# Attention of a two-layer trunk: a written order for three engines, transposes moved into the projection, work moved to GpSimd

## Chip, cores and metric

The kernel runs on one core of a Trainium2 chip. The metric is device time in microseconds of one execution. PE is TensorE, DVE is VectorE, ACT is ScalarE, POOL is GpSimd and SP the queue that starts the transfers.

## What is computed

One attention layer and one convolution layer, each followed by an MLP, over 1024 latent tokens and 256 context tokens (1280 keys in 10 tiles of 128), width 1024. Only the attention is touched. It has two parts whose outputs are projected together:

```python
def diff_attention(q, k, v, lam, lam_init, subln_g):      # 4 heads, two scores each
    s = jnp.einsum('bqhid,bkhid->bhiqk', q, k) * (HEAD_DIM ** -0.5)
    p = jax.nn.softmax(s.astype(jnp.float32), axis=-1)
    attn = (p[:, :, 0] - lam * p[:, :, 1]).astype(v.dtype)
    o = jnp.einsum('bhqk,bkhe->bqhe', attn, v)
    o = rms_norm(o, subln_g) * (1.0 - lam_init)
...
def gqa_attention(q, k, v):                               # 8 query heads, 2 key heads
    s = jnp.einsum('bqgrd,bkgd->bgrqk', q, k) * (HEAD_DIM ** -0.5)
    p = jax.nn.softmax(s.astype(jnp.float32), axis=-1).astype(v.dtype)
    o = jnp.einsum('bgrqk,bkgd->bqgrd', p, v)
```

## The kernel before

All is float32. Where precision is wanted, an operand is split into a rounded high part and a rest (`split`, `sub` at L78: `lo = a - hi`), and the products are summed in PSUM.

The stages follow each other in time: the projection (`project`, to 268 us of the span), the differential attention (268 to 495, with a tail to 513), the grouped attention (513 to 753), then the output projection and the rest of the trunk to the end.

**Projection.** `swept` and `groups` produce keys, queries and values tile by tile in PSUM; `keys_a`, `queries_a`, `rest_b` and `queries_b` turn each tile by its rotary angles (and norm it, in the grouped heads) on DVE and leave it with the tokens on partitions (`kA`, `qA`, `kB`, `qB`).

**Differential attention.** 32 steps: 4 heads of 8 blocks of 128 queries; two steps are a unit (`UnitA`). Of a head's keys, `kstack` transposes ten tiles twice on PE (L1113), ACT copies the high part (L1115), DVE subtracts for the rest (L78); `qstack` does so for 512 queries (L1128, L1131, L1132). A step computes two rows of scores of 128x1280 in three PSUM banks each (`softmax`: L1142, L1143), takes the maximum on DVE (L1145), the exponentials with their sum on ACT (L1148), combines both on DVE into `e0 + cc * e1` (L1261, 128x1280), transposes ten tiles (`transposed`, L1157, copied by ACT at L1162), and every second step multiplies by the values (L1279). Every fourth step `finish` norms 512 columns of the output: a square, two matmuls (L1290, L1291), and `rsqrt0` with DVE's L468 to L470 and L1296; POOL makes the diagonal operand (L1267).

**Grouped attention.** Eight halves of two heads, called j, each of ten key tiles. Per key tile `exponentials` runs four matmuls (L1388, L1389) and two exponentials (L1390) into `pt`; the sum over tiles is added up by POOL for tiles 1 to 6 and by DVE for 7 to 9 (L1394, 128x1024); `values` runs four matmul records (L1403) two tiles later. `ahead` computes the next j's maxima in eight pieces of three matmuls (L1362) and three reductions (L1364), one piece per tile, and writes each into `w` (L1365), which `shifts` transposes and copies (L1371, L1375, L1377). `divide` sums over partitions on PE (L1418), inverts on ACT (L1421, L1422) and multiplies on DVE (L1423 to L1425).

**Order.** Nothing in these stages is written in engine order: Tile's scheduler places every instruction by the priority in which `build` issues it, moved by `high_priority(offset=...)`. PSUM holds two score tiles of three banks (later five of one bank and the values' own) and two banks named `one` for everything else. Scratch of 128x512 comes from a pool `u` of 23 buffers, exponentials from one of 6.

## Time and profile before

| what | value |
|---|---|
| median of three executions | 2577.77 us (2576.82 to 2579.6) |
| profiled execution | 2576.91 us |
| its span, first to last instruction | 2575.1 us |
| mean granted TensorE clock | 0.974 |
| PE, DVE, ACT, POOL busy, share of the span | 95%, 73%, 48%, 13% |

A row of a list of groups reads: line, engine, operation, output and inputs with their shapes, count, then busy microseconds and mean nanoseconds of one, then idle time of the engine ahead of them and what ended it. A row of a timeline reads: start and duration in microseconds, engine, line, operation, count, and in brackets the idle time before it. Matmuls overlap in the pipeline, so the distance from one start to the next is their cost, and the duration of a group is a little longer than that. PE carries two or four records for a float32 operation of full precision.

### The profile page before, as it was taken

The page shows a single profiled execution, that of the slowest core. Times are in us where ns is not written, and L with a number is a line of the kernel's source. Part 1 is how long each engine was busy: PE and PEld are TensorE (multiplying, and loading weights), DVE is VectorE, ACT ScalarE, POOL GpSimd, SP SyncE. Part 2 cuts the span into 40 slices and gives each one's busy share as a digit, 9 for nine tenths or more (in the row PEclk, how much of TensorE's full clock was granted, in tenths as well). Part 3 has the DMA queues.
Part 4 walks back from the last instruction along what each step waited for, and adds up shares of the span by engine and source line. Part 5 has one row for each costly group of instructions (what it writes and reads, how often), then busy time and mean ns, then how long its engine had stood idle before and what let it go on. Part 6 is the DMA issues. An engine that isn't in the chain of part 4 may idle for free. (4 is left out here: it accounts for less than half of the span.)

```text
span 2575.1 us, 30269 instructions
## 1 busy us (share of the span) xinstructions
PE 2435.0 (95%) x10950; PEld 1895.7 (74%) x10950; DVE 1891.7 (73%) x2925; ACT 1225.9 (48%) x1986; POOL 345.2 (13%) x230
## 2 busy tenths in 40 slices
PE   7999899999999979999899999999999999899997
PEld 5888677744447767787688777788777888688786
DVE  4847888887768787876756689767887565765867
ACT  3113577755542475554344346534258555344343
POOL 0001000044442410000000033001231000000002
PEclk9999899999999989999899999999999999899999
DMA  7811011000011057877542221123213444843231
GB/s 271 288 52 46 21 21 46 15 16 6 1 66 50 21 177 250 258 270 257 197 150 88 94 103 33 58 82 120 102 33 126 141 151 160 308 136 132 88 117 66
DMA packets 118519, 297.15 MB, mean 115 GB/s; under 512 B 13536, under 2 KB 19296, under 8 KB 118368
## 3 DMA queue, kind: packets, MB, share of 16 engines
q1 hardware_dynamic: 118368, 295.20, 34.2%
q8 instruction: 86, 1.41, 0.2%
q14 instruction: 65, 0.53, 0.1%
HBM read 225.29 MB, written 63.96 MB: 112 GB/s over the span
## 5 line engine op out<-in xcount | busy, mean ns | idle before, releaser
L74 PE MATMUL ps<-bl,part 128*128 128x512 f32 x784 | 309.7, 396 | 7.0 <-DVE bl L78 7.0
L73 PE MATMUL ps<-bh,part 128*128 128x512 f32 x784 | 310.4, 397 | 6.2 <-ACT part L916 6.2
L75 PE MATMUL ps<-bh,part 128*128 128x512 f32 x784 | 308.7, 396 | 5.8 <-DVE part L78 5.8
L916 ACT CAST part<-a 128x512 fp32r<-128x512 f32 x196 | 121.7, 623 | 306.5 <-PE ps L74 159.8
L78 DVE TENSOR_TENSOR part<-a,part 128x512 fp32r<-128x512 f32 x196 | 134.7, 690 | 162.1 <-ACT part L916 162.1
L73 PE MATMUL ps<-T,a 128*128 128x512 f32 x608 | 238.6, 392 | 6.4 <-DVE tmp L825 3.6
L74 PE MATMUL ps<-T,a 128*128 128x512 f32 x608 | 237.5, 391 | 2.2 <-DVE T L78 2.2
L75 PE MATMUL ps<-T,a 128*128 128x512 f32 x608 | 237.2, 390 | 0.0
L536 POOL TENSOR_TENSOR acc<-acc,mb 128x512 f32<-128x512 f32 x29 | 48.1, 1688 | 1070.6 <-ACT mb L533 1070.6
L73 PE MATMUL ps<-H,a 128*128 128x512 f32 x456 | 178.5, 392 | 3.7 <-ACT a L540 3.7
L74 PEld LDWEIGHTS ps<-bl,part 128*128 128x128 f32 x784 | 150.2, 192 | 41.1 <-DVE bl L78 9.2
L78 DVE TENSOR_TENSOR a<-raw,a 128x1024 fp32r<-128x1024 f32 (+1 forms) x114 | 119.2, 1047 | 83.3 <-PE ps L74 72.5
L75 PEld LDWEIGHTS ps<-bh,part 128*128 128x128 f32 x784 | 150.3, 192 | 38.7 <-DVE part L78 7.2
L73 PEld LDWEIGHTS ps<-bh,part 128*128 128x128 f32 x784 | 149.8, 191 | 39.3 <-ACT part L916 7.4
L74 PE MATMUL ps<-H,a 128*128 128x512 f32 x456 | 177.9, 390 | 0.0
L75 PE MATMUL ps<-H,a 128*128 128x512 f32 x456 | 177.7, 390 | 0.0
L540 ACT CAST a<-raw 128x1024 fp32r<-128x1024 f32 (+1 forms) x114 | 100.9, 908 | 136.2 <-PE ps L74 94.6
L825 DVE TENSOR_TENSOR tmp<-ps,tmp 128x512 f32<-128x512 f32 x114 | 78.4, 689 | 116.0 <-PE ps L75 80.2
L73 PEld LDWEIGHTS ps<-T,a 128*128 128x128 f32 x608 | 114.4, 188 | 35.3 <-DVE tmp L825 6.2
L74 PEld LDWEIGHTS ps<-T,a 128*128 128x128 f32 x608 | 114.4, 188 | 26.6 <-DVE T L78 3.6
L75 PEld LDWEIGHTS ps<-T,a 128*128 128x128 f32 x608 | 114.6, 188 | 23.9
L1390 ACT ACTIVATE pt<-s 128x512 f32<-128x512 f32 x160 | 92.7, 596 | 81.0 <-PE s L1389 72.1
(414 smaller groups left out, 5907.0 us busy)
## 6 DMA issues: line engine op xcount, KB each, us to landing
gq<-tmp SPq DMA_DIRECT2D x196, 256.0 KB, 3.4
b<-gq SPq DMA_DIRECT2D x98, 512.0 KB, 3.3
raw<-in_w SPq DMA_DIRECT2D x72, 512.0 KB, 4.2
a<-in_w SPq DMA_DIRECT2D x140, 256.0 KB, 5.1
raw<-in_adaT SPq DMA_DIRECT2D x48, 512.0 KB, 5.0
adar<-in_adaT SPq DMA_DIRECT2D x32, 512.0 KB, 5.0
raw<-in_cw_in SPq DMA_DIRECT2D x24, 512.0 KB, 3.6
ada<-in_adaN SPq DMA_DIRECT2D x16, 512.0 KB, 8.4
```

The source lines that it names most:

```text
L73: mm(ps, lhsT=lh, rhs=rh, start=start, stop=False, **kw)
L74: mm(ps, lhsT=lh, rhs=rl, start=False, stop=False, **kw)
L75: mm(ps, lhsT=ll, rhs=rh, start=False, stop=stop, **kw)
L78: return eng.tensor_tensor(out=out, in0=a, in1=hi.bitcast(F32), op=ALU.subtract)
L536: self.eng(NORM[li, h]["sub"][j]).tensor_tensor(out=a, in0=a, in1=mb, op=ALU.subtract)
L540: self.nc.scalar.copy(out=hi, in_=src)
L825: nc.vector.tensor_tensor(out=o, in0=a, in1=b, op=op)
L916: self.tc.keep_in_program_order(nc.scalar.copy(out=hi, in_=src))
L1390: nc.scalar.activation(pt[:, s, :], o, AF.Exp)
```

## The change

1. `keys_a`, `queries_a`, `rest_b` and `queries_b` now transpose their tile at once (`turned`: up to four PE transposes of 128x128 into a bank `one`, and as many ACT copies), 114 transposes in all, into `kT`, `qT`, `kB`, `qB` with the tokens along the row. `kstack` and `qstack`, with 164 transposes, are gone; `keys` and `queries` read SBUF. The rest of a differential key moves from DVE to POOL.
2. From the end of the projection to the end of the attention the order on PE, ACT and DVE is the one in which the code issues (`manual_schedule`).
3. The combination is cut by groups of 512, 512 and 256 columns: DVE does the first, POOL the other two, each as a scaling (TENSOR_SCALAR) and an addition (TENSOR_TENSOR). Steps 30 and 31 stay with DVE.
4. The norms of the differential heads leave that stage. The unscaled output is kept, and each of the eight norms runs during one j of the grouped part, with one float32 matmul instead of two, four small scalings and one addition on POOL for the diagonal, and four DVE instructions.
5. The grouped part goes in rounds of two key tiles; the values of a round stand together in the next one, eight records in a row; one reduction writes all of `w`; the addition of key tile 7 moves from DVE to POOL; the four loads of the first output weights are spread.
6. The buffers: `u` 30 instead of 23, exponentials 7 instead of 6.

The core of the diff:

```diff
+        def turned(src, outs):
+            tr = self.one()
+            for h in range(4):
+                nc.tensor.transpose(tr[:, h * P:(h + 1) * P], src[:, h * P:(h + 1) * P], self.ident)
+            for h in range(4):
+                nc.scalar.copy(out=outs[h], in_=tr[:, h * P:(h + 1) * P])
...
         def queries_a(t, z):
-            rope_to(z, t - NC, 8, [(self.qA[h][:, t - NC, :], h * P, P) for h in range(4)], tmp(), tmp())
+            q = tmp()
+            rope_to(z, t - NC, 8, [(q, 0, 512)], tmp(), tmp())
+            turned(q, [self.qT[h][:, (t - NC) * P:(t - NC + 1) * P] for h in range(4)])
...
+            nc.scalar.copy(out=k1[r, c:c + m * P], in_=a)
+            t.sub(nc.gpsimd, k2[r, c:c + m * P], a, k1[r, c:c + m * P])
...
-        nc.vector.scalar_tensor_tensor(out=e0, in0=e1, scalar=cc, in1=e0, op0=ALU.mult, op1=ALU.add)
+            if g == 0 or n >= 30:
+                nc.vector.scalar_tensor_tensor(out=a, in0=b, scalar=cc, in1=a, op0=ALU.mult, op1=ALU.add)
+            else:
+                nc.gpsimd.tensor_scalar(out=b, in0=b, scalar1=cc, scalar2=1.0, op0=ALU.mult, op1=ALU.mult)
+                nc.gpsimd.tensor_tensor(out=a, in0=a, in1=b, op=ALU.add)
...
+                    for g in (1, 2)[:1 + (k - 3) % 2]:
+                        self.transposes(k - 3, g)
+                        self.copies(k - 3, g)
+                if b:
+                    self.scores(k, 1)
+                if 0 <= k - 1 < n:
+                    self.combine(k - 1)
+                if c:
+                    self.transposes(k - 2, 0)
+                if b:
+                    self.exponentials(k, 0)
+                if c:
+                    self.copies(k - 2, 0)
+                if b:
+                    self.exponentials(k, 1)
+                if k >= 4:
+                    self.values((k - 4) // 2, k % 2)
...
+                for m in range(8):
+                    at(5 * j + m // 2, m % 2, lambda j=j, m=m: self.maximum(j + 1, m // 2, m % 2))
+                later(5 * j + 4, 0, lambda j=j: self.shifts(j + 1), 1)
+            if j < 6:
+                at(5 * j + 2, 2, lambda j=j: self.queries(j + 2))
...
+            later(5 * j + 3, 0, norm, 5, 7, 9)
+            later(5 * j + 6, 2, lambda j=j: self.divide(j), 2, 4)
...
-            eng = nc.gpsimd if kt < 7 else nc.vector
+            eng = self.nc.gpsimd if kt < 8 else self.nc.vector
```

(`at(r, place, f)` puts f behind the first tile, behind the second, or at the end of round r; `later` puts the parts that f returns the given number of places on.)

DVE in the differential attention, a step in mid-stage before. L1145 takes a row's maximum, L1266 and L1258/L1259 make factors of one column, L1261 is the combination, L1132 belongs to `qstack`.

```order
L1132 SCALAR_TENSOR_TENSOR q_3176<-one,q_3176 64x512
L1145 TENSOR_REDUCE mx<-s 128x1 x2
L1266 TENSOR_TENSOR c_3233<-sm 128x1
L1145 TENSOR_REDUCE mx<-s 128x1
L1258 RECIPROCAL cc<-sm 128x1
L1259 SCALAR_TENSOR_TENSOR cc<-cc,sm,nlam 128x1
L1261 SCALAR_TENSOR_TENSOR e<-e,cc 128x1280
```

The same place now (L1158 is the maximum, L1176 the combination, L1144 the queries' rest):

```order
L1176 SCALAR_TENSOR_TENSOR e<-e,cc 128x512
L1144 SCALAR_TENSOR_TENSOR q_4034<-qT_1349,q_4034 64x512
L1144 SCALAR_TENSOR_TENSOR q_4035<-qT_1349,q_4035 64x512
L1158 TENSOR_REDUCE mx<-s 128x1 x2
L1171 RECIPROCAL cc<-sm 128x1
L1172 SCALAR_TENSOR_TENSOR cc<-cc,s_2788,nlam 128x1
```

Both maxima of a step now stand together, the combination has 512 columns instead of 1280, and the queries come from SBUF. POOL there, which had one small L1267 per step before, now (L1178 scales, L1179 adds, L78 is a key's rest):

```order
L78 TENSOR_TENSOR k_2953<-kT,k_2952 64x256
L1178 TENSOR_SCALAR e<-e,cc 128x512
L1178 TENSOR_SCALAR e<-e,cc 128x256
L1179 TENSOR_TENSOR e<-e 128x512
L1179 TENSOR_TENSOR e<-e 128x256
L78 TENSOR_TENSOR k_3016<-kT,k_3015 64x512
```

Two scalings and two additions a step, and in six steps of a head a key's rest, have come to POOL. DVE in the grouped attention, one j, before:

```order
L1423 TENSOR_TENSOR ra<-one,r 128x512
L1365 TENSOR_REDUCE w<-mx_6026 128x1
L1364 TENSOR_REDUCE mx_6049<-s 128x1 x3
L1424 SCALAR_TENSOR_TENSOR r<-ra,r 128x512
L1365 TENSOR_REDUCE w<-mx_6049 128x1
L1425 SCALAR_TENSOR_TENSOR ot<-ot,r 128x512
L1364 TENSOR_REDUCE mx_6087<-s 128x1 x3
L1352 SCALAR_TENSOR_TENSOR q_6062<-one,q_6062 64x512
L1365 TENSOR_REDUCE w<-mx_6087 128x1
L1394 TENSOR_TENSOR e<-e,pt 128x1024 x2
L1377 CAST q_5823<-one 64x512
L1352 SCALAR_TENSOR_TENSOR q_6063<-one,q_6063 64x512
```

And now (L1376 maxima, L1246 to L1249 the norm, L1362 the queries' rest, L1446 to L1448 the division, L1413 the additions):

```order
L1413 TENSOR_TENSOR e<-e,pt 128x1024 x2
L1376 TENSOR_REDUCE mx_5538<-s 128x1 x9
L1246 TENSOR_TENSOR dg<-dg,one 128x512
L1247 TENSOR_SCALAR dg<-dg 128x512
L1248 TENSOR_TENSOR sq<-sq,dg 128x512
L1249 SCALAR_TENSOR_TENSOR ot<-ot,subg,sq 128x512
L1376 TENSOR_REDUCE mx_5538<-s 128x1 x9
L1362 SCALAR_TENSOR_TENSOR q_5672<-qB_2261,q_5672 64x512
L1362 SCALAR_TENSOR_TENSOR q_5673<-qB_2261,q_5673 64x512
L1376 TENSOR_REDUCE mx_5538<-s 128x1 x3
L1446 TENSOR_TENSOR ra<-one,r 128x512
L1447 SCALAR_TENSOR_TENSOR r<-ra,r 128x512
```

The norm stands between the maxima of the third and the fourth piece, in each j; the queries' rest now reads two operands from SBUF. DVE at the end of the attention, before, where `spread` (L202) makes the gate's rows that PE transposes ahead of the output projection:

```order
L1394 TENSOR_TENSOR e<-e,pt 128x1024 x3
L202 COPY spread<-m_63 128x128 x8
L1423 TENSOR_TENSOR ra<-one,r 128x512
L1424 SCALAR_TENSOR_TENSOR r<-ra,r 128x512
L78 TENSOR_TENSOR hl<-ot,hh 128x512
L1425 SCALAR_TENSOR_TENSOR ot<-ot,r 128x512
```

And now:

```order
L1413 TENSOR_TENSOR e<-e,pt 128x1024 x2
L1246 TENSOR_TENSOR dg<-dg,one 128x512
L1247 TENSOR_SCALAR dg<-dg 128x512
L1248 TENSOR_TENSOR sq<-sq,dg 128x512
L1249 SCALAR_TENSOR_TENSOR ot<-ot,subg,sq 128x512
L1446 TENSOR_TENSOR ra<-one,r 128x512
L1447 SCALAR_TENSOR_TENSOR r<-ra,r 128x512
L1448 SCALAR_TENSOR_TENSOR ot<-ot,r 128x512
L202 COPY spread<-m_63 128x128 x8
```

The eight `spread` copies stand behind the last norm and the last division.

## Rows read from the trace of the kernel before

**Rows 1.** Busy time by stage: stretch, length, each engine with its instructions, clock

```profile
268.00:495.00 227.00, 208.89 (x1089) 163.79 (x1088) 197.47 (x273) 171.56 (x306) 16.11 (x36) 0.96 0.11 27
495.00:513.00 18.00, 17.96 (x90) 14.07 (x91) 16.08 (x38) 8.10 (x15) 0.40 (x1) 1.00 0.05 10
513.00:753.00 240.00, 236.59 (x913) 112.80 (x911) 182.59 (x310) 129.57 (x228) 117.44 (x51) 1.00 0.03 10
```

**Rows 2.** Groups by form in the differential attention, 300 to 490 us

```profile
L1145 DVE TENSOR_REDUCE mx<-s 128x1 f32<-128x1280 f32 x54 | 79.9, 1484 | 7.6 <-PE s L1143 7.2
L1148 ACT ACTIVATE e<-s,mx 128x1280 f32<-128x1280 f32 x54 | 71.9, 1332 | 11.9 <-DVE mx L1145 11.1
...
L1261 DVE SCALAR_TENSOR_TENSOR e<-e,cc 128x1280 f32<-128x1280 f32 x27 | 41.9, 1550 | 0.8
```

**Rows 3.** PE's timeline in the differential attention, 380 to 391 us

```profile
381.73 1.02 PE L1291 MATMUL one<-dg,sepsm 128*128 128x512 f32 x2
382.59 1.89 PE L1279 MATMUL one<-pt,vA 128*128 128x256 f32 x8
384.32 0.60 PE L1157 MATMUL one<-ident,e 128*128 128x128 f32 x4
...
388.00 1.06 PE L1157 MATMUL one<-ident,e 128*128 128x128 f32 x8
388.81 0.47 PE L1143 MATMUL s<-k,q 128*128 128x512 f32 x1
...
389.81 0.39 PE L1142 MATMUL s<-k,q 128*128 128x512 f32 x1
...
390.97 0.59 PE L1279 MATMUL one<-pt,vA 128*128 128x256 f32 x2
```

**Rows 4.** Groups by form on POOL, whole span

```profile
L675 POOL TENSOR_TENSOR acc<-acc,y 128x512 f32<-128x512 f32 x11 | 19.0, 1745 | 110.1 <-DVE y L88 110.1
...
L78 POOL TENSOR_TENSOR wlo<-wraw,whi 128x512 fp32r<-128x512 f32 x8 | 10.3, 1300 | 212.7 <-ACT whi L230 212.6
...
L1313 POOL MEMSET w<- 128x512 f32 x2 | 1.0, 526 | 0.0
```

**Rows 5.** PE's timeline at the end of the projection

```profile
246.16 0.64 PE L1113 MATMUL one<-ident,kA 128*64 128x128 f32 x2 [3.99 <-DVE k L78]
```

**Rows 6.** Busy time in the sixth and the eighth j of the grouped attention

```profile
676.00:705.00 29.00, 28.91 (x118) 14.47 (x116) 22.95 (x42) 16.08 (x28) 14.18 (x6) 1.00 0.00 1
...
729.00:753.00 24.00, 24.00 (x96) 9.55 (x94) 11.24 (x14) 12.78 (x24) 14.59 (x6) 1.00 0.07 22
```

**Rows 7.** Groups by form in the grouped attention, 510 to 740 us

```profile
L1394 POOL TENSOR_TENSOR e<-e,pt 128x1024 f32<-128x1024 f32 x37 | 88.6, 2394 | 22.9 <-ACT pt L1390 22.4 <-DVE mx L1364 0.3
...
L1394 DVE TENSOR_TENSOR e<-e,pt 128x1024 f32<-128x1024 f32 x21 | 27.5, 1311 | 1.2 <-ACT pt L1390 0.3
...
L1424 DVE SCALAR_TENSOR_TENSOR r<-ra,r 128x512 f32<-128x512 f32 x6 | 16.3, 2723 | 0.0
```

**Rows 8.** DVE's timeline in the eighth j

```profile
742.15 0.69 DVE L1423 TENSOR_TENSOR ra<-one,r 128x512 f32<-128x512 f32 x1 [12.48 <-ACT r L1422]
742.88 2.79 DVE L1424 SCALAR_TENSOR_TENSOR r<-ra,r 128x512 f32<-128x512 f32 x1
...
752.17 1.17 DVE L202 COPY spread<-m 128x128 f32<-128x128 f32 x8
```

**Rows 9.** POOL's timeline in the eighth j

```profile
742.75 5.16 POOL L1394 TENSOR_TENSOR e<-e,pt 128x1024 f32<-128x1024 f32 x2 [0.18 <-ACT pt L1390]
```

**Rows 10.** PE's timeline in the grouped attention and behind it

```profile
640.46 1.08 PE L1403 MATMUL pv<-pt,vB 128*64 128x512 f32 x4
641.47 0.50 PE L1388 MATMUL s<-q,k 128*128 128x512 f32 x1
...
749.91 2.80 PE L1403 MATMUL pv<-pt,vB 128*64 128x512 f32 x12
...
757.77 2.87 PE L73 MATMUL ps<-hid,wfh 128*128 128x512 f32 x5 [1.71 <-ACT hid L540]
```

More of the change, by code (lines that the diff above doesn't have):

```diff
@@ L450, in project @@
             if t == 3:
-                self.at.units[0].prepare()
+                for s, g in ((0, 0), (0, 1), (0, 2), (1, 0), (1, 1), (1, 2)):
+                    self.at.keys(0, s, g)
+                self.at.queries(0, 0)
         pps.__exit__(None, None, None)
@@ new lines, in transposes, with copies @@
+    def transposes(self, n, g):
+        g0, gn = GROUPS[g]
+        tr = self.tr[n, g] = self.one()
+        for i, m in enumerate((n,) if gn == 4 else (n - 1, n)):
+            for k in range(gn):
+                c = (i * gn + k) * P
+                self.nc.tensor.transpose(tr[:, c:c + P], self.e[m, 0][:, (g0 + k) * P:(g0 + k + 1) * P], self.t.ident)
+    def copies(self, n, g):
+        gn = GROUPS[g][1]
+        pt = self.pt.setdefault(n // 2, [])
+        tr = self.tr.pop((n, g))
+        if gn == 4:
+            if n % 2 == 0:
+                pt.append(self.pl.tile([P, gn, 256], F32, name="pt", tag="pt", bufs=8))
+            self.nc.scalar.copy(out=pt[g][:, :, n % 2 * P:(n % 2 + 1) * P], in_=tr.rearrange("p (k q) -> p k q", q=P))
+        else:
+            pt.append(self.t.ut("pt").rearrange("p (k q) -> p k q", k=gn))
+            self.nc.scalar.copy(out=pt[g].rearrange("p k (i q) -> p k i q", i=2), in_=tr.rearrange("p (i k q) -> p k i q", i=2, k=gn))
@@ new lines, in values @@
+    def values(self, u, half):
+        t, nc = self.t, self.nc
+        h, b = u // 4, u % 4
+        pt = self.pt[u]
+        if half == 0:
+            self.pv = self.one()
+        pv = self.pv
+        for kt in range(half * 5, half * 5 + 5):
+            nc.tensor.matmul(pv[:, 0:256], lhsT=t.vA[kt][:, h * P:(h + 1) * P], rhs=pt[kt // 4][:, kt % 4, :],
+                             start=kt == 0, stop=kt == KT - 1)
+        if half == 1:
+            if b == 0:
+                t.oT.append(t.qo.tile([P, T], F32, name="ot", tag="qo"))
+            nc.scalar.copy(out=t.oT[h][:, b * 256:(b + 1) * 256], in_=pv[:, 0:256])
@@ new lines, in misc @@
+    def misc(self, n):
+        h, i = divmod(n, 8)
+        if i == 0:
+            self.queries(h, 1)
+        if h < 3:
+            for s, g in {1: [(0, 0)], 2: [(0, 1)], 3: [(0, 2)], 4: [(1, 0)], 5: [(1, 1)], 6: [(1, 2)]}.get(i, ()):
+                self.keys(h + 1, s, g)
+            if i == 5:
+                self.queries(h + 1, 0)
+        elif i in (3, 4, 5):
+            if i == 3:
+                self.grouped = Grouped(self)
+            self.grouped.keys(0, i - 3)
+        elif i == 6:
+            self.grouped.queries(0)
+            self.t.w_first = []
+        elif i == 7:
+            self.t.first_weights(0)
@@ L1164, in build @@
     def build(self):
         t = self.t
[L1166 to L1168 removed]
+        self.s0 = self.pl.tile([P, 32], F32, name="s0")
+        self.epsi = self.pl.tile([P, P], F32, name="epsi")
+        self.nc.gpsimd.tensor_scalar(out=self.epsi, in0=t.ident, scalar1=P * EPS, scalar2=1.0, op0=ALU.mult, op1=ALU.mult)
+        n = 32
         psa = t.pool("ps2", space=PSUM)
         self.pp = psa.__enter__()
[L1172 to L1177 removed]
@@ L1201, in build @@
-        for k in range(n + 4):
-            if k == n:
-                psa.__exit__(None, None, None)
-                psb = t.pool("ps3", space=PSUM)
-                self.grouped.pp = psb.__enter__()
-            for f, offset in ((prepare, 200), (weights, 100), (scores, None), (values, 0), (finish, 0)):
-                if offset is None:
-                    f(k)
-                else:
-                    with t.tc.high_priority(offset=offset):
-                        f(k)
-            if k >= n:
-                self.grouped.first(k - n)
@@ new lines, in build @@
+        E = mybir.EngineType
+        with t.tc.manual_schedule(engines={E.PE, E.Activation, E.DVE}):
+            for k in range(n + 4):
+                if k == n:
+                    psa.__exit__(None, None, None)
+                    psb = t.pool("ps3", space=PSUM)
+                    self.grouped.pp = psb.__enter__()
+                a, b, c = 0 <= k - 3 < n, k < n, 0 <= k - 2 < n
+                if b:
+                    self.scores(k, 0)
+                if a:
+                    for g in (1, 2)[:1 + (k - 3) % 2]:
[11 more added lines that the diff above has]
+                    self.copies(k - 2, 0)
+                if b:
+                    self.exponentials(k, 1)
+                if k >= 4:
+                    self.values((k - 4) // 2, k % 2)
+                if b:
+                    self.misc(k)
+                else:
+                    self.grouped.first(k - n)
+            self.grouped.build()
```

430 lines of the change are left out of this document (192 added, 238 removed).

## Prediction

> **What bounds the kernel now.** I read the busy time by stage first. PE is busy for 209 of 227 us in the differential attention, 236.6 of 240 in the grouped one [rows 1]: the second waits for nothing but PE, the first has 18 us of PE idle. Behind the attention the order on PE, POOL and SP stays what it was, so that the time can change only up to some 766 us of the span.
>
> In the groups by form of the differential attention, 54 maxima in 190 us are 27 steps [rows 2], 7.04 us each. Over the stage a step has 6.5 us of PE (208.89 over 32), 6.2 of DVE and 5.4 of ACT [rows 1]. No engine is full: the step is longer than each, since two PSUM buffers of scores go round PE, DVE and ACT, and the maxima idle for PE, the exponentials for the maxima [rows 2].
>
> **The change part by part.** The sum stands against the profiled execution, 2576.9 us; the median of the runs shown is 0.9 higher.
>
> *A, the projection.* 114 transposes of 0.10 us (eight from 388.00 to the next start at 388.81 [rows 3]) are 11.5 us on a PE that is full there. Out go the first head's 28 transposes ahead of its scores, 3, and PE's wait for DVE's rest of a key, 4.0 [rows 5], which now is POOL's. New is that the tiles' transposes wait for DVE's rotation; its price is between 0 (PE works ahead on other tiles) and the 4.0 of the nearest wait [rows 5]. With a little under half of it: +6, between +4 and +9.
>
> *B, the 32 steps.* After the change a step has on PE two times six score matmuls of 1.16 us (389.81 to 390.97), ten transposes of 0.10, and ten value records of 0.216 (eight from 382.59 to 384.32) [rows 3]: 2.32 + 1.0 + 2.2 = 5.5, taken as 5.8 with the switches. On DVE: two maxima of 1.48, 0.62 of the combination (1.55 for 1280 columns, by columns [rows 2]), some 0.6 of small ones and queries: 4.2. ACT stays near 5. On POOL: the addition of 512 columns at 1.30 (two operands, `wlo`) [rows 4], 0.65 for half as many; the scaling is not in the trace, and lies between 0.53, the price of a fill of the same shape, and 1.30 of two operands [rows 4]. I take 0.6, since it reads one operand, and 0.35 for 256. A key's rest is 0.8 per step spread over a head (four of 512 columns and two of 256 in eight steps), and DVE's combination holds POOL up once, 0.6. Together 4.3, between 4.2 and 5.4. PE is then the longest at 5.8. Four filling steps at 5 and 28 at 5.8 are 182 in place of 227: **-45**. The cover is POOL's time below PE's, and that the combination has a step and a half until its transposes.
>
> *C, the stage's end.* DVE works for 16 of the 18 us between the last scores and the grouped part [rows 1], mostly on the first j's maxima. In the written order these stand behind the last two combinations (1.55 each [rows 2]), and `shifts` behind all. +5, between 0 and +8.
>
> *D, the grouped part.* PE first. A j takes 29.0 us, 28.9 of them PE [rows 6]. The values in rows of eight save their switch: four records cost 1.01 alone and 0.86 in a row (a third of 12 records less the overlap) [rows 10], 0.8 in five rounds; the queries' transposes go, 0.4; the norm's mean comes, 0.86 (381.73 to 382.59 [rows 3]). That is 28.6, and 22 in the last j, which takes 24 without maxima [rows 6]. If nothing waits, the part takes 7 x 28.6 + 22 = 222, 18 less.
>
> Then DVE. The eighth j shows a wait that the grouped part will have more of. While POOL adds two tiles, 742.75 to 747.9 [rows 9], DVE's L1424 takes 2.79 for work of 0.69, which is what L1423 took just before [rows 8]. It ends when the first addition of 2.39 has ended: the two take turns, and each DVE instruction waits for a whole one of POOL. L1424 does so in every j: 2.72 in the mean [rows 7], a wait of 2.03. L1423, which reads PSUM and one operand from SBUF, does not wait; those that wait read both from SBUF. Before, five instructions per j are of the kind: the three additions, which come when POOL has finished and take 1.31 [rows 7], and two of the division. Now there are nine: three of the norm, two of the queries' rest (whose first operand was PSUM), two of the division, two additions. POOL has more too: seven additions of 2.39 [rows 7], and the norm's diagonal (four scalings of 128 columns, put at 0.45 each, a third of a two-operand addition of 512, and one addition of 1.30 [rows 4]), 3.1: 19.8 per j in place of 14.2 [rows 6], and its queue is filled from the second round to the last. DVE's own work is 22.95 [rows 6], less one addition of 1.31, less the wait of 2.03, plus four of the norm at 0.69: 22.4, and 22 as `w` takes one reduction for eight. With the share of POOL's work in a j of length j as the chance that an instruction has to wait: j = 22 + 9 x 2.03 x 19.8 / j, so j = 33. Following one j by hand through the written order gives the same: PE waits about 2 us for the fourth piece, whose maxima stand behind the norm, 1 for scores behind the queries, and 3 for `shifts` behind the additions. PE can't go round these waits any more. 7 x 33 + 22 = 253 against 240: **+13**. Bounds are 222 (no wait) and 7 x 40 + 22 = 302 (each of the nine waits).
>
> The Trainium skill ("SBUF — State Buffer", section "Who interferes with whom") says that DVE shares its second pair of SBUF ports with GpSimd, and that whoever issues first gets that pair for the whole instruction while the other fully blocks. Read as arrival at any moment, an instruction would wait half of POOL's, 1.2, and only as often as POOL is busy: 22 + 9 x 0.6 x 1.2 = 28.5, no more than PE's own j. The row of 2.79 shows a whole wait instead, for a POOL with work queued; but it is one place in the j, so this is the first rival.
>
> *E, the end.* The eight `spread` copies (1.17 from 752.17 [rows 8]) ran ahead of the last division and now stand behind it and the last norm; the output projection, which began at 757.77 on ACT's `hid` [rows 10], begins later by these and the transposes behind them. +3, between +1 and +6.
>
> The sum: 6 - 45 + 5 + 13 + 3 = -18, and 2576.9 - 18 = 2559, the forecast.
>
> **The rivals.**
>
> *Waits in the grouped part stay small.* For it: DVE's additions took 1.31 in the mean before [rows 7], so they hardly waited, and DVE has 6 us of slack in a j [rows 6]. Against it: POOL's queue is now full when the queries and the division come. With j = 29.5 (28.6 and a little), D is 7 x 29.5 + 22 - 240 = -11, and the time 2535.
>
> *The turn-taking decides, and the kernel is slower.* The place is DVE's queue between the second and the fourth round, where norm, queries and division come one behind the other while POOL always has an addition waiting: each waits whole. The gain of the other parts, 6 - 45 + 5 + 3 = -31, is used up at 7j + 22 = 271, j = 35.6, so with about 6.7 of the nine waiting. With j = 38 (eight waiting) D is +48, and the time 2594. For it: 742.88 [rows 8]. Against it: turns also slow POOL, so that it empties at the end of a j.
>
> *POOL bounds the differential steps.* L675's additions of 512 columns took 1.75 beside a busy DVE [rows 4]. With this for scalings and additions and half of it for 256 columns, a step has 5.2 + 0.8 + 0.6 = 6.6 on POOL, and 28 steps cost 0.8 more each than forecast: 2559 + 22 = 2581, and 2590 if the keys are as dear.
>
> *The steps don't get shorter.* PE in a written order waits at each place for the latest of POOL's sums, ACT's copies and PSUM's two score tiles. If the 7.04 was the round through the two tiles [rows 2] and not the engines' load, it stays: 28 x 1.24 = 35 more, 2594. Against it: both maxima and exponentials now come without the 1.55 of the combination between them.
>
> **How the numbers follow.** Forecast 0.38, small waits 0.22, turn-taking 0.18, POOL 0.08, no shorter steps 0.14. A difference under 0.2%, 5 us, can hardly be told from none in this kernel. Forecast and small waits together give 0.57 of faster, 0.03 within; of the other 0.40 some 0.06 still end faster, 0.09 within, 0.25 slower. Faster 0.63, same 0.12, slower 0.25. The low end is the forecast with D at no wait (-18 in place of +13) and A and C at their lower bounds: 2576.9 + 4 - 45 + 0 - 18 + 3 = 2521, with a little of B taken as 2518. The high end is that of the two slow rivals, 2596. The forecast's own range is 2545 to 2571.
>
> **What would show it.** Right: a step of 5.8 us between maxima of the same kind, PE over 95% busy there, the first grouped scores near 479 of the span in place of 513; in the grouped part instructions of DVE with 2.0 us over their own time, five or six per j, and PE idle behind the maxima and `shifts`, j of 33. Wrong: a step at 7, with POOL full (rival three) or idle (rival four); a j below 30 with DVE's norm at 0.7 each; a scaling on POOL outside 0.53 to 1.30; an output projection that begins as soon after the last values as before.

## Result and the profile after

The changed kernel takes 2613.85 us in the median of four executions (2607.54 to 2618.66), the kernel before 2577.36 beside it: a ratio of 1.0138, 95% interval 1.0116 to 1.0161. It is slower; the forecast was 2559, its range 2518 to 2596, and the time lies above it. The profiled execution, the fastest of the four, took 2607.54 us with a span of 2605.8, PE busy for 93% of it in place of 95%.

The gain came where it was expected, at half the size, and the loss came in three other places. The bounds are first and last rows: of the maxima of the differential steps, of the grouped scores that feed exponentials (L1405), of the sums over partitions (L1438).

| stretch, us of the profiled span | before | after | difference | forecast |
|---|---|---|---|---|
| A: start to the first maximum | 271.4 | 299.3 | +27.9 | +6 |
| B: first to last maximum | 222.1 | 199.6 | -22.5 | -45 |
| C: to the first grouped scores | 19.1 | 28.2 | +9.1 | +5 |
| D: to the last sum | 240.4 | 258.9 | +18.5 | +13 |
| E: to the end | 1822.1 | 1819.8 | -2.3 | +3 |

The last stretch runs the same instructions in all kernels and came out between 1819.8 and 1830 in the runs below, so that a difference of a few us in it tells nothing, and a time is judged by its ratio.

Busy time by stage, after (columns as in [rows 1], which they answer to):

```profile
100.00:299.00 199.00, 175.37 (x905) 146.72 (x904) 120.59 (x294) 56.55 (x219) 17.57 (x14) 0.96 0.24 74
299.00:499.00 200.00, 179.45 (x969) 152.16 (x968) 151.87 (x183) 149.79 (x265) 135.68 (x149) 0.97 0.11 25
499.00:527.00 28.00, 23.23 (x100) 16.72 (x100) 21.52 (x40) 11.47 (x20) 0.00 (x0) 0.94 0.06 19
527.00:786.00 259.00, 230.17 (x886) 112.80 (x885) 197.27 (x267) 139.84 (x252) 171.59 (x99) 0.95 0.04 11
```

PE, which had next to no idle time in the projection and the grouped part before, now idles for 23.6 us in the first row and 28.8 in the last.

**A.** PE's waits from 100 to 300 us, after (line waited, for what: us in all, times, longest), then the only row for 100 to 272 us before:

```profile
PE one L418 <- DVE tmp L364: 15.1, 8, 5.3
PE one L446 <- DVE tmpk L364: 7.0, 6, 3.0
PE one L418 <- ACT tmp L425: 1.1, 1, 1.1
```

```profile
PE one L1113 <- DVE k L78: 4.0, 1, 4.0
```

These are 15 waits of PE at the new transposes, 23.2 us: 14 for DVE's rotation and one for ACT's copy of a context tile. DVE's timeline of two query tiles before, and then after:

```profile
259.91 0.76 DVE L356 TENSOR_TENSOR tmp<-tmp,rs 128x256 f32<-128x256 f32 x2
260.59 0.68 DVE L383 TENSOR_REDUCE ss<-tmp 128x8 f32<-128x512 f32 x1
261.19 0.68 DVE L358 TENSOR_TENSOR tmp<-tmp,rc 128x512 f32<-128x512 f32 x1
...
264.19 0.76 DVE L356 TENSOR_TENSOR tmp<-tmp,rs 128x256 f32<-128x256 f32 x2
```

```profile
257.68 0.76 DVE L358 TENSOR_TENSOR tmp<-tmp,rs 128x256 f32<-128x256 f32 x2
...
259.20 0.69 DVE L364 TENSOR_TENSOR tmp<-tmp 128x512 f32<-128x512 f32 x1
259.81 0.68 DVE L385 TENSOR_REDUCE ss<-tmp 128x8 f32<-128x512 f32 x1
...
262.18 0.23 DVE L86 SCALAR_TENSOR_TENSOR ssa<-ss,eps,ssa 128x8 f32<-128x8 f32 x1 [1.49 <-ACT ssa L85]
...
263.58 0.76 DVE L358 TENSOR_TENSOR tmp<-tmp,rs 128x256 f32<-128x256 f32 x2
```

Before, the next tile's reduction (L383) stood inside this tile's rotation, and a tile took 4.3 us (264.19 - 259.91). After, it stands behind it, DVE then waits 1.49 for ACT, and a tile takes 5.9. PE, held at the transposes, came late to the first scores (293.01 in place of 268.24):

```profile
285.84 1.09 PE L418 MATMUL one<-ident,tmp 128*128 128x128 f32 x4 [4.51 <-DVE tmp L364]
292.27 1.09 PE L418 MATMUL one<-ident,tmp 128*128 128x128 f32 x4 [5.34 <-DVE tmp L364]
293.01 0.78 PE L1155 MATMUL s<-k,q 128*128 128x512 f32 x1
```

**B.** Eight steps in the middle of the stage, what PE waited for most from 347 to 445 us (16 steps), and POOL's scaling from 300 to 480 us:

```profile
396.10:444.65 48.55, 45.86 (x258) 39.59 (x257) 36.81 (x45) 38.97 (x69) 36.70 (x41) 1.00 0.13 28
```

```profile
PE s L1155 <- ACT e L1164: 4.5, 4, 1.5
```

```profile
L1178 POOL TENSOR_SCALAR e<-e,cc 128x512 f32<-128x512 f32 x28 | 32.7, 1168 | 56.5 <-DVE cc L1172 44.6 <-ACT pt L1198 11.9
...
L1178 POOL TENSOR_SCALAR e<-e,cc 128x256 f32<-128x256 f32 x27 | 13.7, 508 | 0.0
```

A step is 48.55 / 8 = 6.07 us. PE is busy for 5.73 of it (94%) and waits for 0.34, mostly until ACT's exponentials have read a tile of scores. POOL is idle for a quarter of the time. Its scaling of 512 columns took 1.17, but that is not its own time. DVE's combination, which reads two operands from SBUF, starts just ahead of it; a step after the change, and then one of e5 (below) where no combination runs beside the scaling (x2 is the scaling of 512 and of 256 columns):

```profile
399.79 0.75 DVE L1176 SCALAR_TENSOR_TENSOR e<-e,cc 128x512 f32<-128x512 f32 x1
399.86 1.70 POOL L1178 TENSOR_SCALAR e<-e,cc 128x512 f32<-128x512 f32 x2 [0.45 <-DVE cc L1172]
```

```profile
417.21 1.15 POOL L1178 TENSOR_SCALAR e<-e,cc 128x512 f32<-128x512 f32 x2 [0.61 <-DVE cc L1172]
```

The scaling of the 512 columns took 1.25 of the first and 0.69 of the second.

**C.** DVE's maxima of the first j, behind the last two combinations:

```profile
508.72 6.20 DVE L1376 TENSOR_REDUCE mx<-s 128x1 f32<-128x512 f32 x12 [1.88 <-PE s L1374]
...
517.11 6.20 DVE L1376 TENSOR_REDUCE mx<-s 128x1 f32<-128x512 f32 x12 [0.75 <-PE s L1374]
```

**D.** PE's two longest sums of waits in the grouped part, DVE's groups there, and the place where one j hands over to the next on PE:

```profile
PE one L1385 <- DVE w L1379: 13.6, 6, 2.6
PE s L1374 <- DVE mx L1376: 10.2, 8, 1.7
```

```profile
L1248 DVE TENSOR_TENSOR sq<-sq,dg 128x512 f32<-128x512 f32 x7 | 15.4, 2195 | 0.2
L1362 DVE SCALAR_TENSOR_TENSOR q<-qB,q 64x512 fp32r<-64x512 f32 x12 | 13.4, 1113 | 1.5 <-ACT q L1360 1.2
L1448 DVE SCALAR_TENSOR_TENSOR ot<-ot,r 128x512 f32<-128x512 f32 x7 | 12.7, 1811 | 0.2
L1447 DVE SCALAR_TENSOR_TENSOR r<-ra,r 128x512 f32<-128x512 f32 x7 | 10.3, 1472 | 0.2
```

```profile
644.57 1.94 PE L1422 MATMUL pv<-pt,vB 128*64 128x512 f32 x8
...
650.24 0.66 PE L1385 MATMUL one<-ident,w 128*128 128x128 f32 x4 [2.61 <-DVE w L1379]
...
652.28 3.00 PE L1422 MATMUL pv<-pt,vB 128*64 128x512 f32 x8
```

The instructions with two SBUF operands take 0.4 to 1.5 us more than their own 0.69, and the last maxima and `w` stand behind them. L1247, which reads one operand from SBUF, waits too (804 ns, and 427 in e12 below). Behind five of the six waits for `w` PE's clock is lower for a while: here eight value records took 3.00 in place of 1.94.

The values' copies part one j from the next. In the middle of the stage they are 34.2 us apart, the last two 22.7. One j after the change, and then one of e12 (below), where POOL adds no key tiles:

```profile
661.60:695.80 34.20, 29.75 (x115) 14.74 (x116) 27.07 (x37) 17.69 (x33) 21.29 (x13) 0.95 0.00 1
```

```profile
648.90:678.00 29.10, 28.00 (x115) 14.39 (x116) 22.29 (x37) 17.55 (x33) 3.45 (x5) 1.00 0.00 1
```

DVE is busy for 27.1 of the 34.2, 4.8 more than without POOL's additions, and idle for the other 7.1: it is not full.

### The profile page after: what moved, and what is told of

Its sections match the earlier page's. It is cut to its first block, busy times and chain, and to the rows that moved or that the text cites. A ratio compares the mean times of both kernels' runs of the same rounds, so it can differ in the third digit from the quotient of the medians.

```text
span 2605.8 us, 30302 instructions
## 1 busy us (share of the span) xinstructions
PE 2412.5 (93%) x10884; PEld 1892.8 (73%) x10884; DVE 1872.9 (72%) x2761; ACT 1238.0 (48%) x2080; POOL 526.2 (20%) x395
## 5 line engine op out<-in xcount | busy, mean ns | idle before, releaser
L78 DVE TENSOR_TENSOR part<-a,part 128x512 fp32r<-128x512 f32 x196 | 134.8, 690 | 157.5 <-ACT part L921 157.4
L78 DVE TENSOR_TENSOR a<-raw,a 128x1024 fp32r<-128x1024 f32 (+1 forms) x114 | 119.6, 1050 | 82.9 <-PE ps L74 72.6
L73 PEld LDWEIGHTS ps<-T,a 128*128 128x128 f32 x608 | 114.1, 188 | 34.2 <-DVE tmp L830 4.6
L1407 ACT ACTIVATE pt<-s 128x512 f32<-128x512 f32 x160 | 86.8, 595 | 109.7 <-PE s L1406 109.1
L74 PEld LDWEIGHTS ps<-T,a 128*128 128x128 f32 x608 | 114.1, 188 | 27.4 <-DVE T L78 4.3
L74 PE MATMUL ps<-hid,w 128*128 128x512 f32 (+1 forms) x336 | 127.4, 380 | 4.3 <-POOL hid L78 2.4
```

The source lines that it names most:

```text
L73: mm(ps, lhsT=lh, rhs=rh, start=start, stop=False, **kw)
L74: mm(ps, lhsT=lh, rhs=rl, start=False, stop=False, **kw)
L78: return eng.tensor_tensor(out=out, in0=a, in1=hi.bitcast(F32), op=ALU.subtract)
L1407: nc.scalar.activation(pt[:, s, :], o, AF.Exp)
```

## Experiments

**The late tiles' transposes alone** (A). The last four query tiles' transposes move into the second to fifth step.

```diff
-            turned(q, [self.qB[h][:, t * P:(t + 1) * P] for h in range(4)])
+            outs = [self.qB[h][:, t * P:(t + 1) * P] for h in range(4)]
+            if t < 4:
+                turned(q, outs)
+            else:
+                self.at.late.append(lambda: turned(q, outs))
```

> Edit: the transposes of the last four grouped query tiles leave the projection and stand in steps 1 to 4 of the differential attention. Theory one (PE, in order, waits at those transposes for DVE's rotation): the waits of 2.1, 4.5, 5.3 and 2.9 us at L418 go, the first scores start near 282 of the span in place of 293.0, the step and the grouped part stay, and the time falls by 9 to 14, to some 2601. Rival (the chain of the last query tiles through ACT and DVE, 5.9 to 6.4 us a tile, holds the first maxima whatever PE does): the first maximum stays later than 296 of the span, and the gain is under 4.

Ratio 1.013 [1.011, 1.0151]; the first maximum came at 297.0, 2.3 earlier. PE reached its first scores sooner, at 286.59, and waited there 6.30 us in one piece, until just behind DVE's scaling of a query tile (L388, which ended at 294.09; PE went on at 294.19). With these transposes out of the way DVE's chain of query tiles held the start.

**All keys and queries of the grouped part transposed late** (A). They are kept as rows, as before, and transposed in place in the steps.

```diff
-            zn, q = headnorm(z, 8, tmp()), tmp()
-            rope_to(zn, t, 8, [(q, 0, 512)], tmp(), zn)
-            turned(q, [self.qB[h][:, t * P:(t + 1) * P] for h in range(4)])
+            zn = headnorm(z, 8, tmp())
+            rope_to(zn, t, 8, [(self.qB[h][:, t * P:(t + 1) * P], h * P, P) for h in range(4)], tmp(), zn)
...
+        if n >= 4 and n % 8 != 7 and self.late:
+            x, c0, m = self.late.pop(0)
+            tr = self.one()
+            for y in range(m):
+                self.nc.tensor.transpose(tr[:, y * P:(y + 1) * P], x[:, c0 + y * P:c0 + (y + 1) * P], self.t.ident)
+            self.nc.scalar.copy(out=x[:, c0:c0 + m * P], in_=tr[:, 0:m * P])
```

> Edit: grouped queries and keys stay in rows in the projection, as before the change, and are transposed in place in steps 4 to 15 of the differential attention (eleven times up to four transposes and one copy). Theory one (the 42 transposes make PE wait for ACT's and DVE's work on each tile, some 19 us in all, and so delay the next tile's products, which start that work): PE's waits at these lines go, the first maximum comes between 275 and 284 in place of 299, the steps lose 1 to 4, and the time falls by 14 to 22, to about 2596. Rival (DVE has more work or POOL's share of the keys slows it): the first maximum stays later than 290 and the gain is under 8.

Ratio 1.0055 [1.004, 1.007], 21 us less than the changed kernel's 1.0138. The first maximum came at 278.6 and the steps stayed at 198.6. DVE's timeline has the reduction inside the rotation again, and of PE's 15 waits at the transposes two are left, this one and 1.2 for ACT:

```profile
266.60 0.68 DVE L385 TENSOR_REDUCE ss<-tmp 128x8 f32<-128x512 f32 x1
267.19 0.68 DVE L360 TENSOR_TENSOR tmp<-tmp,rc 128x512 f32<-128x512 f32 x1
```

```profile
PE one L418 <- DVE tmp L364: 1.3, 1, 1.3
```

So the scheduler fills the rotation from the next tile where its result goes straight to rows, and did not where it goes to PE; why it chose so is not shown.

**POOL out of the combination, and the norms back in the steps** (B). First all of the combination on DVE, then seven norms spread over the steps again, in the written order.

```diff
-            if g == 0 or n >= 30:
+            if True:
```

> Edit: DVE does all three groups of the combination in every step, POOL none. Theory one (the step of 6.07 is PE's 5.7 and small waits, DVE has room): DVE goes from 4.3 to 5.2 us per step, the step stays at 6.0 to 6.2, the time within 5 us of the changed kernel's. Rival A (PE waits for POOL's sums): the step falls to 5.8, 8 us faster. Rival B (taking the combination from DVE is what shortened the step from 7.04): the step rises to 6.6 or more, 15 to 20 us slower.

```diff
+                if k >= 8 and (k - 8) // 4 < 7:
+                    m, i = divmod(k - 8, 4)
+                    if i == 0:
+                        self.parts = self.norm(m)
+                    self.parts[i]()
...
-            later(5 * j + 3, 0, norm, 5, 7, 9)
+            if j >= 7:
+                later(5 * (j - 7) + 3, 0, norm, 5, 7, 9)
```

> Edit: seven of the eight norms go back to the differential stage, each spread over four steps there in the written order; the eighth stays in the first j. Theory one (DVE has 1.7 us of room per step there, none in the grouped part): the step stays under 6.3, up to 6 us more in that stage, the grouped part loses 18 to 25, net 14 to 22 faster than the changed kernel. Rival (turn-taking with POOL's combination costs as much there): the step rises to 6.7 or more, and the net is within 6 of the changed kernel.

Without POOL: 1.0118 [1.0097, 1.014], the steps 193.1, that is 6.5 shorter than with it; PE's waits for ACT's exponentials from 300 to 490 us fell from 14.3 to 9.0. With the norms back: 1.0208 [1.0184, 1.0232], the steps 221.4, nearly the 222.1 of before, the grouped part 249.8. So the norms' leaving is worth 21.8, as much as the whole gain of B, and POOL's share costs 6.5. The rest of the change in this stage, the transposes of keys and queries that left it and the written order (4.5, e5 below), makes up for that; what the transposes alone are worth no run shows.

**No norm, and no written order** (D). The norm left out of the grouped part; then the scheduler's order everywhere.

```diff
-            later(5 * j + 3, 0, norm, 5, 7, 9)
```

> Edit: the norms of the differential heads are left out altogether (that part of the computation is missing). Theory one (DVE's norm, which takes turns with POOL, and POOL's share of it make PE wait for maxima and for w): a j falls from 32.4 us to 28.5 to 29.5, the time by 20 to 28. Rival (the waits come from the written order and the additions, with or without the norm): a j stays at 31 or more, and only the matmuls and a little are saved, under 10.

```diff
-        with t.tc.manual_schedule(engines={E.PE, E.Activation, E.DVE}):
+        with contextlib.nullcontext():
```

> Edit: the changed kernel without the written order; the scheduler places PE, ACT and DVE in the attention, all else stays. Theory one (the start's loss lies in the projection, which no written order covers; in the grouped part the written order makes PE wait in front of w, about 2.3 us and a lower clock behind it per j): the first maximum stays near 299, the steps get longer than 6.07 (6.3 to 7), the grouped part gets shorter by 5 to 15; the whole within 15 of the changed kernel. Rival (the written order is what costs at the start too): first maximum before 290.

Without the norm, which e3 leaves out: 1.0132 [1.0115, 1.015], the grouped part 250.9, only 8 shorter. Without the order: 1.0095 [1.008, 1.011]; the stage's end is 19.2 as before the change, the steps 4.5 longer, and the grouped part is 249.3, though PE's waits there, 28 us in the changed kernel, come to 5.3. The last experiments explain that.

**Other places for the same instructions** (D). The division's end and the next queries one round later; then also the norm in single instructions and the queries behind `w`, in e9 (its diff stands behind the first's):

```diff
-                at(5 * j + 2, 2, lambda j=j: self.queries(j + 2))
+                at(5 * j + 4, 2, lambda j=j: self.queries(j + 2))
...
-            later(5 * j + 6, 2, lambda j=j: self.divide(j), 2, 4)
+            later(5 * j + 6, 2, lambda j=j: self.divide(j), 2, 4, 9)
```

> Edit: the last two instructions of the division, and the queries' rest of the next but one j, move to the end of a j's fifth round, where no maxima are. Theory one (what makes PE wait for w is the division in front of the last maxima on DVE, taking turns with POOL): the wait for w of 13.6 us in six j shrinks under 4, a j falls from 32.4 to 29.5 to 30.5, the time by 12 to 20. Rival (the turns go on in the fifth round and hold up w's copy or the next j's maxima): waits move elsewhere, under 6 gained.

```diff
-                at(5 * j + 2, 2, lambda j=j: self.queries(j + 2))
+                at(5 * j + 3, 2, lambda j=j: self.queries(j + 2))
...
-            later(5 * j + 3, 0, norm, 5, 7, 9)
+            later(5 * j + 3, 0, norm, 5, 7, 9, 10, 12, 13)
```

> Edit, in the grouped part alone: the end of the division goes to the fifth round as in the run before, the queries' rest stands behind w in the fourth round, and the norm's four DVE instructions are put one per place instead of four in a row. Theory one (PE waits where a group of turn-taking DVE instructions stands in front of maxima or w, and PE cannot go round it): the waits for maxima, w and queries fall from 24 us in all to under 8, the part from the first scores to the last sums from 258.9 to 235 to 243, the time by 16 to 24. Rival (the turns themselves, nine waits a j wherever they stand, hold DVE): the part stays over 250, under 9 gained.

1.0122 [1.0107, 1.0137] and 1.0111 [1.0096, 1.0126], grouped parts of 247.7 and 249.6, 11 and 9 shorter. In the first the division and the queries' rest took their own 0.69, but PE now waited for the queries themselves, which stand later; in the second the queries (L1368) in their new place took three times their own time, one of the division's two 2.05, and PE waited 16.0 us for maxima:

```profile
PE s L1374 <- DVE q L1362: 9.8, 6, 2.7
```

```profile
L1368 DVE SCALAR_TENSOR_TENSOR q<-qB,q 64x512 fp32r<-64x512 f32 x12 | 25.0, 2082 | 0.4
```

Other places gave back up to a third of what POOL's additions cost here (34, next run). The rest stayed, as waits at other instructions.

**POOL's additions out of the grouped part** (D).

```diff
-            eng = self.nc.gpsimd if kt < 8 else self.nc.vector
-            eng.tensor_tensor(out=f, in0=self.pt[j, 0] if kt == 1 else f, in1=self.pt[j, kt], op=ALU.add)
+            x = self.pt[j, kt]
+            if kt == 8:
+                self.nc.vector.scalar_tensor_tensor(out=f, in0=x, scalar=1.0, in1=x, op0=ALU.add, op1=ALU.add)
+            elif kt == 9:
+                self.nc.vector.tensor_tensor(out=f, in0=f, in1=x, op=ALU.add)
```

> Edit: the changed kernel without the seven additions per j that POOL makes (the softmax sums of the grouped heads then lack those tiles); the norm's small POOL work, the order and all DVE instructions stay, in number and shape. Theory (POOL's additions make nine DVE instructions per j take turns, and their place in the order only decides where PE waits): the division, the queries' rest and the norm take their own time (0.7 us each), the part from first scores to last sums falls from 258.9 to 222 to 234, the time by 25 or more. Rival (the written order by itself, or PE's own work, makes the part long): it stays over 245, under 12 gained.

1.0024 [1.0012, 1.0036]; the grouped part fell to 225.0. DVE has as many instructions as after; the same ones now take:

```profile
L1362 DVE SCALAR_TENSOR_TENSOR q<-qB,q 64x512 fp32r<-64x512 f32 x12 | 8.2, 686 | 4.1 <-ACT q L1360 4.0
L1450 DVE SCALAR_TENSOR_TENSOR r<-ra,r 128x512 f32<-128x512 f32 x7 | 7.1, 1020 | 0.2
...
L1451 DVE SCALAR_TENSOR_TENSOR ot<-ot,r 128x512 f32<-128x512 f32 x7 | 5.1, 734 | 0.2
L1248 DVE TENSOR_TENSOR sq<-sq,dg 128x512 f32<-128x512 f32 x7 | 4.8, 693 | 0.2
```

L1248 fell from 2195 to 693 ns and L1448 (here L1451) from 1811 to 734; L1450, which stands beside POOL's part of the norm, kept a third of a microsecond. PE's waits are 6.5 in place of 28. This is the turn-taking that the forecast had read from [rows 8]. The 33.9 us hold all that the additions cause, the slower clock behind the waits included.

**The pieces put together.** The late transposes, the late division and DVE's combination in the written order (e8); with e9's places and the first maxima spread as well (e10); the first and the last of the three without an order (e11); that with the queries read from PSUM and tile 7 added on DVE (e13).

> Edit: the rows kept in the projection, the late division and queries' rest, and the whole combination on DVE, together. Theory one: the gains add: 18 at the start, 6 in the steps, 16 in the grouped part, 2574 (2565 to 2585), no slower than the kernel before. Rival (what is gained at one place is lost to a wait at the next): over 2595.

> Edit: rows kept in the projection, the combination on DVE, the grouped part of the run above, and the first j's maxima two per step over the last four steps instead of four per step over two. Theory one (the gains add; the stage's end is DVE's twelve reductions in a row): first grouped scores 19 to 23 us after the last maximum in place of 28, the grouped part 235 to 243, the whole 2550 to 2565, faster than the kernel before. Rival (waits move on): 2570 or more.

> Edit: rows kept in the projection and the combination on DVE, and no written order. Theory one (the start's loss comes from the transposes in the projection, and is got back whatever places the attention): first maximum near 279, stage's end 19, grouped part 249 as without the order before, 2574 to 2584. Rival (the scheduler loses elsewhere what the start gains): over 2590.

```diff
-            eng = self.nc.gpsimd if kt < 8 else self.nc.vector
+            eng = self.nc.gpsimd if kt < 7 else self.nc.vector
...
-        tr = t.qB[j // 2][:, j % 2 * 512:(j % 2 + 1) * 512]
+        x = t.qB[j // 2][:, j % 2 * 512:(j % 2 + 1) * 512]
+        tr = self.one()
+        for i in range(4):
+            nc.tensor.transpose(tr[:, i * P:(i + 1) * P], x[:, i * P:(i + 1) * P], t.ident)
```

> Edit, on the version with rows in the projection, DVE's combination and no written order: the grouped queries are transposed by PE when needed and read from PSUM, as in the kernel before, and tile 7's addition is DVE's again. Theory: two of nine turns per j go (one operand in PSUM does not wait), POOL has an addition less, PE four transposes more: the grouped part falls from 249.4 to 241 to 246, the time by 4 to 8, to 2567. Rival (without a written order the turns are hidden behind PE, which is the bound at 249): the part stays within 2, the time too.

1.0005 [0.9994, 1.0016], 1.0004 [0.9992, 1.0016], 0.9982 [0.9967, 0.9997] and 0.9987 [0.9974, 1.0001]. The gains of e2, e6 and e7 add up (0.0119 in the ratio, and 0.0133 in e8). Spreading the first maxima took nothing from the stage's end (26.6 in both), and e10's grouped part was 251.7 where 235 to 243 had been expected. The grouped part of e13 was 251.9 where 249.4 had been: reading the queries from PSUM did not help, and PE's few waits (5.3 us in e5) don't account for the scheduler's 249 either.

**Order in the steps alone, then PE's order in the grouped part.** To e11 the written order is given back for the 32 steps; then, for PE only, in the grouped part; then e7's places on top.

```diff
+            order.enter_context(t.tc.manual_schedule(engines={E.PE, E.Activation, E.DVE}))
             for k in range(n + 4):
                 if k == n:
+                    order.close()
```

> The written order is kept for the 32 steps alone; from the end of the combination part on the scheduler places the work (queries and keys transposed late, combination all on VectorE). Theory: the order earns its gain in the steps and loses it in what follows, and the pieces are independent. Then the steps take 191 to 193 us as with the order everywhere, the stage's end 19 to 21 us as without it, the grouped part 249 to 252 us, the span 2565 to 2570 and the ratio 0.996 to 0.998. Rival: the pieces are not independent, the scheduler has nothing left to fill the last steps and the stage's end with, so the end takes 26 us or more or the grouped part 255 us or more, and the ratio is 1.000 or above.

```diff
+            order.enter_context(t.tc.manual_schedule(engines={E.PE}))
             self.grouped.build()
```

> As the run before (order in the steps, scheduler at the stage's end), but in the grouped part PE alone keeps the written order, and VectorE and ScalarE are placed by the scheduler. Theory: the scheduler's grouped parts stayed at 249 to 254 us without waits on PE because it parts the two value matmuls of a pair (rows of 2 records take as long as rows of 4; 109.7 us of value records in place of 77.5). With PE's own order back the value records take 77 to 85 us, and since VectorE can now go round what is late, the grouped part takes 225 to 240 us and the ratio is 0.988 to 0.995. Rival: the records come down, but the turns of VectorE and GpSimd come back as waits on PE: grouped part 245 to 255 us, ratio 0.996 to 1.000.

> As the run before, with the end of the division and the next queries' rest written one round later, as in e7. Theory: where the scheduler places VectorE the written place decides little, so that the grouped part is within 3 us of the run before. Rival: PE's order is tied to these places, and the grouped part is 4 us or more shorter or longer.

e14: 0.9979 [0.997, 0.9988], steps 191.2 and the stage's end 19.3 as expected, the grouped part 253.9, 2 more than expected. e15: **0.9938 [0.9919, 0.9958]**, 2562.49 us, the grouped part 240.4, at the upper end of the theory's 225 to 240. e16: 0.9937 [0.9918, 0.9957], 242.7, so the places hardly count once DVE may go round them. The value records on PE in e14 and then in e15, each with rows of its timeline:

```profile
L1429 PE MATMUL pv<-pt,vB 128*64 128x512 f32 x320 | 109.7, 617 | 0.0
```

```profile
614.52 1.07 PE L1429 MATMUL pv<-pt,vB 128*64 128x512 f32 x2
...
616.07 1.93 PE L1429 MATMUL pv<-pt,vB 128*64 128x512 f32 x6
```

```profile
L1430 PE MATMUL pv<-pt,vB 128*64 128x512 f32 x320 | 78.0, 608 | 0.0
```

```profile
602.05 1.94 PE L1430 MATMUL pv<-pt,vB 128*64 128x512 f32 x8
```

A value matmul fills 64 of the 128 columns and leaves two records; the one for the other half stands next to it in the program. One alone (x2) takes 1.07, two in a row (x4) 1.08 [rows 10], four (x8) 1.94. The scheduler moves one of the four away from its partner, and the same 320 records take 32 us more of PE. That is what the scheduler's grouped parts lost where PE showed no wait. In e15 PE keeps its rows, and the part is 13.5 shorter than in e14. DVE's turns remain but cost PE less: its waits in the part are 18.3 us, where the changed kernel has 28. A row of the division and PE's longest sum of waits:

```profile
L1455 DVE SCALAR_TENSOR_TENSOR r<-ra,r 128x512 f32<-128x512 f32 x7 | 16.3, 2323 | 0.2
```

```profile
PE s L1382 <- DVE mx L1384: 5.8, 8, 1.8
```

## Why the prediction was wrong

Two terms of the sum failed by 22 us each: in A the price of PE's waits at the new transposes, in B the time of the 32 steps at their two ends. C and D came out 4 and 5.5 above.

**A: +6 between +4 and +9, measured +27.9.** The price of the new wait was bounded by "0 (PE works ahead on other tiles) and the 4.0 of the nearest wait", and 1.5 of it stands in the sum. A single wait bounded one that comes 15 times: the rows add up to 23.2, and with that in place of 1.5 the sum gives +28 (an estimate: 11.5 - 3 - 4.0 + 23.2). PE could not work ahead: what stood behind a transpose waited with it, 4.51 at 285.84 and 5.34 at 292.27. Nor did the forecast see why the waits are long: DVE's own order changed when the rotated tile went to PE, and its period for a query tile went from 4.3 to 5.9. e1 took 16 of the 42 grouped transposes off PE's way and left DVE's order: 2.3 us. e6 took all 42 off and gave DVE its old order: 20.7. How these divide between the other 26 transposes and the order no run shows.

**B: -45, measured -22.5.** Against the same stretch as the forecast's (first scores to last maximum) it is 205.9 (498.9 - 293.0) in place of 182. PE is the longest, as forecast, and its 5.8 a step were right (5.73); with the waits for ACT's exponentials a step is 6.07, and 28 x 0.27 = 7.6. The other 16 lie at the two ends, which the sum had as "four filling steps at 5": 6.3 from the first scores to the first maximum, the first seven steps 48.2 in place of 7 x 6.07 (5.7 more), and the last nine 54.2 where the sum leaves five at 6.07 and the four at 5 (3.9 more). The first seven belong to A's late tiles: in e6 they took 43.2. POOL's scaling at 0.6 and another 0.6 for DVE's combination holding it up are 1.2 in the sum, and measured 1.17 with the wait and 0.69 without. POOL did not become the bound, as the third rival has it, since it was idle for a quarter; but without its share the steps are 6.5 shorter (e2), which the sum had not. That the steps would not get shorter is refuted by the 22.5; of these the norms' leaving alone is worth 21.8 (e4).

**C: +5 between 0 and +8, measured +9.1.** The reason was right: the first j's maxima stand as two blocks of 6.20 us behind the last two combinations, at 508.72 and 517.11. It is the written order, since without it the end takes 19.2 (e5, e11). Spreading them over more steps did not help (e10).

**D: +13, measured +18.5. The wait was the right one, its price and the path to the sum were not, and that the number is near is in part luck.** j was put at 33 and the last one at 22; they are 34.2 in the middle and 22.7. But the formula has j as DVE's load, 22 of its own and 11 of turns. DVE's own is 22.3 (e12), as forecast; the turns add 4.8, under half of their price, and DVE is idle for the rest of j. What makes j long is PE, which in the written order waits for the maxima and `w` that stand behind a turn: 4.5 idle in a j, and 1.7 more for the same work than in e12, where its clock was granted at 1.00 in place of 0.95. That is the prediction's second way, PE's waits followed by hand (6 in a j). The whole of the additions cost 34 (258.9 and 225.0 in e12) where 31 was forecast (253 and 222). The first rival counted half a wait per turn, 6.5 in a j, which is nearer to the 4.8 than the 11. What is refuted is its conclusion, that a DVE with time to spare leaves PE's j as it was. The rule of the Trainium skill ("SBUF — State Buffer", section "Who interferes with whom") that it started from, that one of the two fully blocks, agrees with L1248's 2195 beside POOL and 693 without, and on POOL's side with the scaling's 1.25 beside a combination and 0.69 without. "The turn-taking decides" was right that the kernel is slower, but its price (+48) was not reached.

**E: +3.** The output projection begins 5.5 us behind the last sum (791.48 - 786.0) where it began 4.8 behind it (757.77 - 753.0): +0.7, below the +1 to +6 of the forecast and too small to matter.

By the measured terms the sum is 27.9 - 22.5 + 9.1 + 18.5 - 2.3 = +30.7, the difference of the profiled spans (the medians differ by 36.5). None of the rivals had its place in the projection; the slow side came from a term that had been given a range of 5 us, and from one, B, that had none.

## What to carry to other kernels

A transpose that is moved to where its input is made can put a wait into PE's queue each time: count the waits, not the one nearest in the trace, and look at what the producing engine used to do in that gap. Where DVE and POOL took turns, other places for the same instructions gave back 9 to 11 of 34 us (e7, e9); taking POOL's additions out gave back all of it (e12), and an order that binds PE alone and lets DVE go round what is late 18 (e15). An engine that has time left can still make another wait, if the order puts what the other needs behind a turn. The fastest version has a written order for three engines in the steps and for PE alone, with its pairs, in the grouped part, keeps the grouped rows in the projection and the whole combination on DVE: it ended 0.6% below the kernel before.

## What the runs showed of the hardware

Two matmuls of 64 columns cost as much as one if they stand next to each other: 1.08 for a row of four records, 1.07 for one of two; parted pairs took 32 us more of PE in a part of 254. The kernel before paid for it too: 28 of its 92 rows of value records have two, and they are the larger part of why its values took 100.8 us in the grouped part, against 78.0 in e15, where all rows have eight:

```profile
L1403 PE MATMUL pv<-pt,vB 128*64 128x512 f32 x320 | 100.8, 617 | 0.4 <-ACT pt L1390 0.4
```

POOL's scaling of 128x512 by a value per partition took 0.69 us by itself (e5) and 1.25 when a DVE instruction with two SBUF operands had begun 0.07 us ahead of it: it then ended 0.56 behind that one's end. The group's mean of 1.17 hides both. The granted clock was 1.00 (2.4 GHz) in the 7.6 us ahead of the wait of 2.61 at 650.24, and 0.66 in the mean of the 5.0 us behind it, so at 1.2 GHz for a part of them:

```profile
640.00:647.60 7.60, 7.32 (x30) 3.55 (x26) 7.06 (x9) 5.10 (x10) 7.60 (x7) 1.00 0.00 1
...
650.20:655.20 5.00, 4.96 (x16) 2.02 (x16) 1.56 (x2) 1.77 (x3) 0.44 (x1) 0.66 0.01 3
```
